# A hybrid decoder layer on one core: the linear attention's q and k turned by VectorE blocks and transfers in place of TensorE, with decay products and copies given to GpSimd

## The chip, the core and the metric

The kernel runs on one core of a Trainium2 chip. The metric is device time in microseconds for one execution, the median of several runs. Before the change it is 305.76 us (three runs, 305.73 to 305.92). The engines are called as the profile calls them: PE is TensorE (PEld its weight loads), DVE is VectorE, ACT is ScalarE, POOL is GpSimd, SP is the SyncE that issues most transfers.

## What is computed

One layer of a decoder with 256 tokens and a width of 1024, all in float32. A single input projection of the normed x gives softmax-attention q, k, v (8 heads of 64), linear-attention q, k, v (4 heads, key width 64, value width 128), an output gate r and a rank-16 gate. Both attentions feed one output projection; then comes a gated feed-forward part with a causal convolution of 3 taps, and a last norm. What matters here is the gated linear attention, chunk by chunk of 64 tokens:

```python
def gla_attention(q, k, v, log_a):
    ...
    qc = to_chunks(q * (dk ** -0.5))
    kc, vc = to_chunks(k), to_chunks(v)
    G = jnp.cumsum(to_chunks(log_a), axis=3)
    ...
        diff = G_[:, :, :, None, :] - G_[:, :, None, :, :]
        decay = jnp.exp(jnp.where(causal[None, None, :, :, None], diff, -jnp.inf))
        A = jnp.einsum('bhtd,bhsd,bhtsd->bhts', q_, k_, decay)
        o = (jnp.einsum('bhts,bhsv->bhtv', A, v_)
             + jnp.einsum('bhtd,bhdv->bhtv', q_ * jnp.exp(G_), state))
```

The result o is normed per head (so a common factor on it matters only through a small epsilon), multiplied by a gain and by silu(r).

## The kernel before

**Weights.** Every weight matrix comes in pieces ("slots") of up to 128 x 2048 by SP (L92) into a ring of four raw buffers. Each slot is split into a high part by ACT (split_hi, L99) and a low part by DVE (split_lo, L102), and each product is made of three matmuls (mm3, L115 to L118: high x high, high x low, low x high). When the last low part of a slot is written, split_lo issues the next load on SP (load_next), so loads stand in SP's queue in the order in which low parts are finished.

**Order.** PE, ACT and DVE run in the order in which the program lists their instructions; the order on SP and POOL is left to the scheduler. The input projection is a list of 48 steps of about 1.4 us on PE (for the last 24, six matmuls of 512 columns each): steps 0 to 11 the linear attention's q, k and gate ("G", slots 0, 3, 4, 5) and the first pieces of softmax q and k; 12 to 17 softmax q (slots 6, 7); 18 to 23 softmax k (slots 8, 9); 24 to 31 v (slots 10, 11); 32 to 39 the linear v (slots 12, 13); 40 to 47 r (slots 14, 15); 48 to 63 are the output projection (slots 16 to 19). Everything else hangs on the plan, a table written by hand (L631 to L653): at step q, or at its half (q + 0.5), the functions of that row are emitted, so their PE instructions stand at that place in PE's queue and their ACT and DVE instructions behind those of earlier rows. The feed-forward part behind it (22 blocks of weights) is bound by PE in the same way.

**Linear attention.** At step 12 the rows of G, with tokens on partitions, are scaled by the norm and copied to gqk (g_evac, L274): columns 0 to 255 are q, 272 to 527 k. g_lr_split (L287, L288) and g_wgs_lo (L282) prepare the gate's operands. At 14.5 g_transpose transposes q and k with eight PE instructions of 128 x 128 (L302), so that the channels lie on partitions, and ACT copies them to gqT, with the factor 1/8, and gkT (L303), and k once more to gk1 (L305). g_diag (L309, L311, L314) multiplies q and k, makes id64 and sums the products of each head on DVE; g_diag2 (L320) makes from them the diagonal of the attention matrix ATd on ACT. g_gate_mm (L325), g_gate and g_decay (L341) make the decay of each token, dec[0]. Then the triangle of a chunk is filled by levels: for b = 1, 2, 4 up to 32 lvl_u multiplies q (L355, L356, L362) and k (L363) in place by the decays of half a block, and L364 makes the decays of the next level by products of neighbours. lvl_c (L399) makes a level's products on PE and lvl_d_ (L410) copies them with a mask to ATd. Levels 0 and 1 are multiplied together at step 29; so that later levels may overwrite q and k, their operands are kept aside: q1 and gk1 for level 0, and for level 1 copies by ACT (lvl_keep, L382, L383).

**Softmax attention around it.** rope_a copies the swapped halves of q and k (ACT, L512, to the tile qs) and rope_b rotates them (DVE, L519 to L521). m_scores (L535), m_max (L557), m_exp (L564), m_div (L570 to L572) and m_pt (PE transposes of the probabilities, L581) follow for pairs of heads from step 29 on. masks (L541 to L545) loads and copies the causal mask.

**The form that the change reuses.** In the feed-forward part the kernel already turns a tile by 32 x 32 blocks on DVE (blocks, L913) and then moves whole blocks between partitions by transfers of SP (to_rows, L920), 16 of 32 partitions by 16 runs of 128 bytes.

Of the kernel before, what the change touches and what calls it, by code (L numbers as in the profile page):

```python
# [9 lines left out]
F32 = mybir.dt.float32  # L10
# [24 lines left out]
def trunk_kernel(ctx: ExitStack, tc: tile.TileContext, xT_d, wG_d, w5_d, wo_d, up_d, dn_d,  # L35
# [174 lines left out]
    gqT = at.tile([128, 2, S], F32, name="gqT")  # L210
    gkT = at.tile([128, 2, S], F32, name="gkT")
# [18 lines left out]
    gr = at.tile([128, 2, 512], F32, name="gr")  # L230
# [65 lines left out]
    def g_transpose(which):  # L296
        p = att()
        o, dst, sc = ((0, gqT, DK ** -0.5), (272, gkT, 1.0))[which]
        for pr in range(2):
            for tt in range(2):  # L300
                c = pr * S + tt * 128
                T.transpose(p[:, c:c + 128], gqk[:, tt, o + pr * 128:o + (pr + 1) * 128], ident)  # L302
        A.activation(dst.rearrange("p a t -> p (a t)"), p, AF.Copy, scale=sc)  # L303
        if which:
            A.activation(gk1.rearrange("p a t -> p (a t)"), p, AF.Copy)  # L305

    def g_diag():
        dgp = at.tile([128, 2, 256], F32, name="e", bufs=2)
        V.scalar_tensor_tensor(dgp, gqk[:, :, 0:256], DK ** -0.5, gqk[:, :, 272:528],  # L309
                               op0=ALU.mult, op1=ALU.mult)  # L310
        V.tensor_add(id64, ident[:, 0:64], ident[:, 64:128])  # L311
        dg = at.tile([128, 2, 2, 2], F32, name="dg")
        for tt in range(2):
            V.tensor_reduce(dg[:, :, tt, :], dgp[:, tt].rearrange("p (a h d) -> p a h d", a=2, h=2),  # L314
                            axis=mybir.AxisListType.X, op=ALU.add)
        st["dg"] = dg.rearrange("p a b c -> p (a b c)")
# [22 lines left out]
    def g_decay():  # L339
        V.tensor_sub(st["mn"], st["mn"], st["ln"])  # L340
        A.activation(dec[0], st["mn"], AF.Exp, scale=1.0 / TAU)  # L341

# [9 lines left out]
    def lvl_u(l):  # L352
        b = LEVELS[l]
        if l == 0:
            V.tensor_mul(q1, two(gqf, 1)[:, :, 1, 0], two(dec[0], 1)[:, :, 1, 0])  # L355
# [6 lines left out]
        V.tensor_mul(two(gqf, c)[:, :, 1], q, dc[:, :, 0].to_broadcast([128, n, c]))  # L362
# [812 lines left out]
```

## Time and profile before

| | |
|---|---|
| median of 3 runs | 305.76 us |
| the profiled execution | 306.11 us |
| its span, first to last instruction | 304.1 us |
| granted TensorE clock | 1.000 |
| POOL busy, instructions | 4.8 us, x21 |
| moved by SP's queue | 55.86 MB, 53.1% of 16 engines |

The profile is of one execution. A row of the timeline gives the start and the duration in us, engine, line, operation, tiles and shape, how many were merged, and in brackets the idle time in front and what ended it. A row of a line gives minimum, median and maximum in ns. The chain that ended last is followed back from the last instruction.

### The profile page before, as it was taken

How to read it: one execution, taken by the hardware profiler on the slowest of the kernel's cores; microseconds unless marked ns; L12 is line 12 of the kernel's file. 1: busy time of each engine (PE TensorE's matmuls, PEld its weight loads, DVE VectorE, ACT ScalarE, POOL GpSimd, SP SyncE). 2: the span in 40 equal slices, each digit the busy share in tenths (PEclk: the TensorE clock that was granted, in tenths of full speed). 3: DMA queues.
4: the chain of work that ended last, by engine and by line, in shares of the span. 5: the costliest groups of instructions: out<-in, count | busy, mean ns of one | idle time of the engine just before them, and what ended most of it. 6: DMA issues, size and time to landing. Idle time of an engine off the chain costs nothing.

```text
span 304.1 us, 6224 instructions
## 1 busy us (share of the span) xinstructions
PE 297.7 (98%) x2470; PEld 282.2 (93%) x2470; DVE 248.2 (82%) x464; ACT 207.0 (68%) x384; POOL 4.8 (2%) x21
## 2 busy tenths in 40 slices
PE   8999999999999999999999999999999999999992
PEld 8999988777889999999999999999999999999992
DVE  3788998999387699799999998887888788876653
ACT  3988999898998487657667775555556665534362
POOL 2020000000000000000000000000000000000000
PEclk9999999999999999999999999999999999999999
DMA  6998845274553542991567666448788622220003
GB/s 163 391 332 307 297 165 198 91 261 141 176 182 134 204 168 65 426 370 32 210 245 256 254 235 236 170 156 224 211 194 234 267 71 69 71 69 2 0 0 139
DMA packets 20892, 56.38 MB, mean 185 GB/s; under 512 B 9840, under 2 KB 11648, under 8 KB 16640
## 3 DMA queue, kind: packets, MB, share of 16 engines
q1 hardware_dynamic: 20720, 55.86, 53.1%
q8 instruction: 19, 0.31, 0.4%
q10 hardware_dynamic: 144, 0.13, 0.1%
q14 instruction: 9, 0.07, 0.1%
HBM read 53.89 MB, written 1.05 MB: 181 GB/s over the span
## 4 chain that ended last, share of the span: by engine, by line
PE 98%; ACT 0%; issue 0%; DVE 0%; ACTq 0%
PE att L116 14%; PE att L117 14%; PE att L118 14%; PE acc L116 14%; PE acc L118 14%; PE acc L117 14%; PE att L746 4%; PE acc L727 1%; PE att L77 1%; PE att L399 1%; PE att L535 1%; PE att L581 1%; PE att L463 1%; PE att L601 1%; PE acc L735 1%; PE att L302 0%
## 5 line engine op out<-in xcount | busy, mean ns | idle before, releaser
L99 ACT ACTIVATE hi<-raw 128x1024 fp32r<-128x1024 f32 (+4 forms) x87 | 79.9, 941 | 38.4 <-PE att L117 31.9
L102 DVE TENSOR_TENSOR lo<-raw,hi 128x1024 fp32r<-128x1024 f32 (+4 forms) x89 | 93.6, 1065 | 14.0 <-ACT hi L99 14.0
L116 PE MATMUL att<-hh,hi 128*128 128x256 f32 x352 | 98.4, 279 | 0.0
L117 PE MATMUL att<-hl,hi 128*128 128x256 f32 x352 | 98.3, 279 | 0.0
L118 PE MATMUL att<-hh,lo 128*128 128x256 f32 x352 | 98.2, 279 | 0.0
L116 PEld LDWEIGHTS att<-hh,hi 128*128 128x128 f32 x352 | 66.2, 188 | 0.0
L117 PEld LDWEIGHTS att<-hl,hi 128*128 128x128 f32 x352 | 66.2, 188 | 0.0
L118 PEld LDWEIGHTS att<-hh,lo 128*128 128x128 f32 x352 | 66.2, 188 | 0.0
L873 DVE SCALAR_TENSOR_TENSOR c<-us,par,c 128x256 f32<-128x256 f32 x88 | 40.7, 482 | 4.1 <-ACT c L865 2.5
L865 ACT ACTIVATE c<-us,par 128x256 f32<-128x256 f32 x44 | 24.0, 591 | 23.7 <-DVE us L855 18.4
L118 PE MATMUL acc<-dhi,gl 128*128 128x512 f32 (+1 forms) x88 | 32.1, 365 | 0.0
L117 PE MATMUL acc<-dlo,gh 128*128 128x512 f32 (+1 forms) x88 | 32.1, 365 | 0.0
L116 PE MATMUL acc<-dhi,gh 128*128 128x512 f32 (+1 forms) x88 | 31.9, 363 | 0.0
L815 DVE TENSOR_TENSOR dlo<-draw,dhi 128x1024 fp32r<-128x1024 f32 x22 | 26.6, 1218 | 0.0
L855 DVE TENSOR_TENSOR us<-att,rb 128x512 f32<-128x512 f32 x20 | 13.8, 688 | 11.5 <-PE att L118 11.5
L810 ACT ACTIVATE dhi<-draw 128x1024 fp32r<-128x1024 f32 x22 | 23.0, 1046 | 0.0
L116 PE MATMUL acc<-hi,ah 128*128 128x512 f32 x48 | 19.5, 406 | 0.0
L118 PE MATMUL acc<-hi,al 128*128 128x512 f32 x48 | 19.0, 396 | 0.0
L117 PE MATMUL acc<-lo,ah 128*128 128x512 f32 x48 | 19.0, 396 | 0.0
L117 PEld LDWEIGHTS acc<-dlo,gh 128*128 128x128 f32 x88 | 16.5, 188 | 2.0
L116 PEld LDWEIGHTS acc<-dhi,gh 128*128 128x128 f32 x88 | 16.5, 188 | 1.9
L118 PEld LDWEIGHTS acc<-dhi,gl 128*128 128x128 f32 x88 | 16.5, 188 | 1.9
(222 smaller groups left out, 511.0 us busy)
## 6 DMA issues: line engine op xcount, KB each, us to landing
raw<-in_up SPq DMA_DIRECT2D x22, 1024.0 KB, 4.9
draw<-in_dn SPq DMA_DIRECT2D x22, 512.0 KB, 5.7
raw<-in_w SPq DMA_DIRECT2D x7, 1024.0 KB, 6.8
raw<-in_wo SPq DMA_DIRECT2D x4, 1024.0 KB, 4.8
raw<-in_w SPq DMA_DIRECT2D x4, 512.0 KB, 5.6
raw<-in_wG SPq DMA_DIRECT2D x3, 528.0 KB, 5.8
raw<-in_w SPq DMA_DIRECT2D x4, 256.0 KB, 5.4
xg<-hB SPq DMA_DIRECT2D x16, 64.0 KB, 6.4
```

Of the source, the lines that this page charges most:

```text
L77: T.matmul(wp[:, :w], zero, zero[:, :w], start=True, stop=True)
L99: A.activation(self.hi[:, a:b], self.raw[:, a:b], AF.Copy)
L102: V.tensor_sub(self.lo[:, a:b], self.raw[:, a:b], self.hi[:, a:b])
L116: T.matmul(out, sh, mh, start=first, stop=False, **kw)
L117: T.matmul(out, sh, ml, start=False, stop=False, **kw)
L118: T.matmul(out, sl, mh, start=False, stop=last, **kw)
L746: T.matmul(st["G"][tt][c][:, :c1 - c0], sta[:, k, tt * 128:(tt + 1) * 128], mov[:, kk, c0:c1], start=k == 0 and i == 0, stop=k == KT - 1 a ...
L810: A.activation(hi, downs[i][0], AF.Copy)
L815: V.tensor_sub(lo, d, hi)
L855: V.tensor_tensor(u[:, :, 2:], upo[i][2].rearrange("p (a t) -> p a t", a=2), rb[:, None, :].to_broadcast([128, 2, S]), op=ALU.mult)
L865: A.activation(cv[i][:, a], u[:, a, 2:], AF.Identity, bias=par[:, P_CB + m:P_CB + m + 1], scale=par[:, P_CW + 2 * 2 * NP + m:P_CW + 2 * 2 ...
L873: V.scalar_tensor_tensor(c[:, a], u[:, a, w:w + S], par[:, wc:wc + 1], c[:, a], op0=ALU.mult, op1=ALU.add)
```

## The change

- q and k are turned by two DVE block transposes into gB (g_blocks) and 16 transfers of 32 x 32 blocks into gT (g_turn), even ones on SP's queue, odd ones on POOL's. gqT and gkT are views of gT. The eight PE transposes and ACT's copies of L303 and L305 go; gk1 is copied by POOL (g_keep1).
- q isn't scaled any more; the factor 1/8 goes into the evacuation of the linear v (a DVE instruction makes the scaled norm factors), as the diagonal's products, too, lose it.
- The decay products of all levels move from DVE (L364, L371) to POOL, right behind dec[0]; the kept copies of level 1 (lvl_keep) move from ACT to POOL; the diagonal's multiplication and id64 move from DVE to POOL, and its sums (g_diag1) stay on DVE but move from step 14.5 to 24.
- gB and gr share a buffer (tag "gr").
- The plan is rearranged: g_wgs_lo goes behind slot 7's last low part, the gate from 15.5 to 16, level 0 behind slot 9's last low part, k's half of level 1 to step 20, the loads of lvl and masks from 12.5 to 19, slot 11's second high part to step 24.

```diff
+    def g_blocks():
+        for w, o in enumerate((0, 272)):
+            V.transpose(gB[:, w].rearrange("p r a f -> p a r f"),
+                        gqk[:, :, o:o + 256].rearrange("p a (r f) -> p a r f", r=2))
+
+    def g_turn():
+        src = gB.rearrange("p w r a f -> p (w r a) f")
+        dst = gT.rearrange("p w r (a t) -> p (w r a) t", a=2)
+        for n in range(16):
+            b, c = divmod(n, 4)
+            (nc.gpsimd if n % 2 else DMA).dma_start(dst[32 * b:32 * b + 32, :, 32 * c:32 * c + 32], src[32 * c:32 * c + 32, :, 32 * b:32 * b + 32])
+
+    def g_keep1():
+        nc.gpsimd.tensor_copy(gk1.rearrange("p a t -> p (a t)"), gkf)
...
-        V.scalar_tensor_tensor(dgp, gqk[:, :, 0:256], DK ** -0.5, gqk[:, :, 272:528],
-                               op0=ALU.mult, op1=ALU.mult)
-        V.tensor_add(id64, ident[:, 0:64], ident[:, 64:128])
+        nc.gpsimd.tensor_mul(dgp, gqk[:, :, 0:256], gqk[:, :, 272:528])
+        nc.gpsimd.tensor_add(id64, ident[:, 0:64], ident[:, 64:128])
...
     def g_decay():
         V.tensor_sub(st["mn"], st["mn"], st["ln"])
         A.activation(dec[0], st["mn"], AF.Exp, scale=1.0 / TAU)
+        for l in range(1, 7):
+            dc = two(dec[l - 1], 1)
+            nc.gpsimd.tensor_mul(dec[l], dc[:, :, 0, 0], dc[:, :, 1, 0])
...
     def lvl_keep():
         q, k = keep(1)
-        A.activation(q.rearrange("p (n b) -> p n b", b=2), two(gqf, 2)[:, :, 1], AF.Copy)
-        A.activation(k, gkf, AF.Copy)
+        nc.gpsimd.tensor_copy(q.rearrange("p (n b) -> p n b", b=2), two(gqf, 2)[:, :, 1])
+        nc.gpsimd.tensor_copy(k, gkf)
...
     def gv_evac(tt):
-        A.activation(gv[:, tt], st["gv"][tt], AF.Copy, scale=rstd(tt))
+        if tt == 0:
+            V.tensor_scalar(rsx[:, 2:4], rsx[:, 0:2], DK ** -0.5, None, op0=ALU.mult)
+        A.activation(gv[:, tt], st["gv"][tt], AF.Copy, scale=rsx[:, 2 + tt:3 + tt])
...
-            (12, lambda: do((xnorm, lambda: slots[7].split_lo(0, 512)), (lambda: slots[7].split_lo(512, 1024),), (g_evac, 0), (g_lr_split,), (g_evac, 1), (g_wgs_lo,), (hi, 7, 1), (lo, 7, 1))),
-            (12.5, lambda: do((DMA.dma_start, lvl, lvl_d), (masks,))),
+            (12, lambda: do((xnorm, lambda: slots[7].split_lo(0, 512)), (lambda: slots[7].split_lo(512, 1024),), (g_evac, 0), (g_lr_split,), (g_evac, 1), (g_blocks,), (g_turn,), (hi, 7, 1), (lo, 7, 1), (g_wgs_lo,))),
             (13.5, lambda: do((hi, 8, 0))),
-            (14.5, lambda: do((g_transpose_lr,), (g_transpose, 0), (g_transpose, 1), (xrow,), (lo, 8, 0), (g_diag,))),
-            (15.5, lambda: do((g_gate_mm,), (g_gate,), (hi, 9, 0), (g_decay,), (lo, 9, 0), (hi, 9, 1))),
-            (16.5, lambda: do((lvl_u, 0), (lo, 9, 1), (lvl_u, 1))),
-            (18, lambda: do((rope_a, 0, 0), (rope_b, 0, 0), (hi, 10, 0), (lo, 10, 0), (rope_a, 0, 1), (rope_b, 0, 1), (hi, 10, 1), (lo, 10, 1))),
-            (20, lambda: do((hi, 11, 0), (lo, 11, 0), (hi, 11, 1), (lvl_keep,), (DMA.dma_start, glag, gla_g_d))),
-            (24, lambda: do((lvl_u, 2), (rope_a, 1, 0), (rope_b, 1, 0), (lo, 11, 1), (rope_a, 1, 1), (rope_b, 1, 1), (hi, 12, 0), (lo, 12, 0), (g_diag2, 0), (g_diag2, 4))),
+            (14.5, lambda: do((g_transpose_lr,), (xrow,), (lo, 8, 0))),
+            (16, lambda: do((g_gate_mm,), (g_gate,), (hi, 9, 0), (g_decay,), (lo, 9, 0), (hi, 9, 1), (g_keep1,), (g_diag,))),
+            (18, lambda: do((lo, 9, 1), (lvl_u, 0), (lvl_u, 1, (0,)), (rope_a, 0, 0), (rope_b, 0, 0), (hi, 10, 0), (lo, 10, 0), (rope_a, 0, 1), (rope_b, 0, 1), (hi, 10, 1), (lo, 10, 1))),
+            (19, lambda: do((DMA.dma_start, lvl, lvl_d), (masks,), (DMA.dma_start, glag, gla_g_d))),
+            (20, lambda: do((hi, 11, 0), (lvl_u, 1, (1,)), (lvl_keep,), (lo, 11, 0))),
+            (24, lambda: do((lvl_u, 2), (rope_a, 1, 0), (rope_b, 1, 0), (hi, 11, 1), (lo, 11, 1), (rope_a, 1, 1), (rope_b, 1, 1), (hi, 12, 0), (lo, 12, 0), (g_diag1,), (g_diag2, 0), (g_diag2, 4))),
```

In lvl_u the new argument parts picks q's multiplication (0), k's (1) or both.

More of the change, by code (lines that the diff above doesn't have):

```diff
@@ L209, in trunk_kernel @@
     gqk = at.tile([128, 2, NG], F32, name="gqk")
-    gqT = at.tile([128, 2, S], F32, name="gqT")
-    gkT = at.tile([128, 2, S], F32, name="gkT")
+    gT = at.tile([128, 2, 2, S], F32, name="gT")
+    gqT, gkT = gT[:, 0], gT[:, 1]
+    gB = at.tile([128, 2, 2, 2, 128], F32, name="gB", tag="gr")
     gk1 = at.tile([128, 2, S], F32, name="gk1")
@@ L229, in trunk_kernel @@
     gv = at.tile([128, 2, 512], F32, name="gv")
-    gr = at.tile([128, 2, 512], F32, name="gr")
     glag = at.tile([128, 512], F32, name="glag")
@@ L294, in g_transpose_lr, with g_diag1 @@
         A.activation(lrT, p[:, :S], AF.Copy)
[L296 to L305, printed above, removed]
+    def g_blocks():
[10 more added lines that the diff above has]
+        nc.gpsimd.tensor_copy(gk1.rearrange("p a t -> p (a t)"), gkf)
     def g_diag():
         dgp = at.tile([128, 2, 256], F32, name="e", bufs=2)
-        V.scalar_tensor_tensor(dgp, gqk[:, :, 0:256], DK ** -0.5, gqk[:, :, 272:528],
-                               op0=ALU.mult, op1=ALU.mult)
-        V.tensor_add(id64, ident[:, 0:64], ident[:, 64:128])
+        nc.gpsimd.tensor_mul(dgp, gqk[:, :, 0:256], gqk[:, :, 272:528])
+        nc.gpsimd.tensor_add(id64, ident[:, 0:64], ident[:, 64:128])
+        st["dgp"] = dgp
+    def g_diag1():
+        dgp = st["dgp"]
         dg = at.tile([128, 2, 2, 2], F32, name="dg")
@@ L350, in two, with lvl_u @@
         return x.rearrange("p (n two b) -> p n two b", two=2, b=b)
-    def lvl_u(l):
+    def lvl_u(l, parts=(0, 1)):
         b = LEVELS[l]
@@ L361, in lvl_u @@
         q = q1.rearrange("p (n c) -> p n c", c=1) if l == 1 else two(gqf, c)[:, :, 1]
-        V.tensor_mul(two(gqf, c)[:, :, 1], q, dc[:, :, 0].to_broadcast([128, n, c]))
-        V.tensor_mul(two(gkf, c)[:, :, 0], two(gkf, c)[:, :, 0], dc[:, :, 1].to_broadcast([128, n, c]))
-        V.tensor_mul(dec[l], dc[:, :, 0, 0], dc[:, :, 1, 0])
+        if 0 in parts:
+            V.tensor_mul(two(gqf, c)[:, :, 1], q, dc[:, :, 0].to_broadcast([128, n, c]))
+        if 1 in parts:
+            V.tensor_mul(two(gkf, c)[:, :, 0], two(gkf, c)[:, :, 0], dc[:, :, 1].to_broadcast([128, n, c]))
     def lvl_u64():
@@ L370, in lvl_u64 @@
         V.tensor_mul(two(gkf, c)[:, :, 0], two(gkf, c)[:, :, 0], dc[:, :, 1].to_broadcast([128, 8, c]))
-        V.tensor_mul(dec[6], dc[:, :, 0, 0], dc[:, :, 1, 0])
         d6 = dec[6].rearrange("p (a b c) -> p a b c", a=2, b=2)
@@ L490, in g_gated @@
         y = st["y", tt]
-        V.tensor_mul(y, y, gr[:, tt])
+        V.tensor_mul(y, y, st["gr"][:, tt])
     def g_out():
```

4 lines of the change are left out of this document (3 added, 1 removed).

## The prediction

> **What bounds the kernel now.** I read the page first, then the chain of waits in order of time, then who waited for whom on TensorE, then the timeline of each engine from 20 to 62 us, where the change acts.
>
> ```profile
> span 304.1 us, 6224 instructions
> PE 297.7 (98%) x2470; PEld 282.2 (93%) x2470; DVE 248.2 (82%) x464; ACT 207.0 (68%) x384; POOL 4.8 (2%) x21
> PE 98%; ACT 0%; issue 0%; DVE 0%; ACTq 0%
> PE att L77 <- PEq L1164: 0.8, 1, 0.8
> ```
>
> The third line is the chain that ended last: it is TensorE (PE) almost alone. The fourth is the only wait that the profile has for matmuls on PE, at the launch. So PE runs without a hole from the first matmul to the end. Time can be gained only by taking instructions from PE, and any hole put into PE is lost for good, because nothing behind it has slack to give back. I therefore keep one number through the working: s, by how much PE is later than before (negative: earlier). The s that PE has when the attention part is over is the change of the total.
>
> **What leaves PE.** Before, q and k of the linear attention are transposed by eight PE instructions (L302). They stand between two others:
>
> ```profile
> 26.99 1.06 PE L302 MATMUL att<-ident,gqk 128*128 128x128 f32 x8
> 27.89 0.38 PE L265 MATMUL att<-ident,rsx 128*128 128x128 f32 x2
> 29.51 0.40 PE L325 MATMUL att<-lrT,wgs 128*128 128x256 f32 x2
> 29.75 0.28 PE L116 MATMUL acc<-ah,hi 128*128 128x256 f32 x1
> 29.87 0.28 PE L117 MATMUL acc<-al,hi 128*128 128x256 f32 x1
> ```
>
> From 26.99 to 27.89 is 0.90 us: s can become -0.90 and no better. That alone is 0.29% of the time. Everything else in the change can only hide or cost.
>
> **What VectorE gets in exchange, and the first wait.** The blocks are turned by two VectorE (DVE) instructions, each of the form that the kernel already has at L913:
>
> ```profile
> 25.95 0.23 DVE L288 TENSOR_TENSOR lrs<-gqk,lrs 128x64 fp32r<-128x64 f32 x1
> 26.21 0.85 DVE L282 TENSOR_TENSOR wgs<-wgu,wgs 16x256 fp32r<-16x256 f32 x2
> 27.34 1.23 DVE L102 TENSOR_TENSOR lo<-raw,hi 128x1024 fp32r<-128x1024 f32 x1 [0.28 <-ACT hi L99]
> L913 DVE STREAM_TRANSPOSE hB<-xg x4: 703/704/707, 175.3 to 199.1; 128x512 f32<-128x512 f32 x4
> ```
>
> They start where L282 stood, at 26.2, and end at 26.2 + 2 x 0.70 = 27.6. The low part of slot 7 follows (1.2, to 28.75), and only then, because the change moves it to the end of the list, L282 (0.85, to 29.6). L282 writes the wgs that the gate's matmul L325 reads. That matmul moves from half step 15.5 to step 16, six matmuls of 0.117 later (the last two rows are 0.12 apart), so with 0.90 less in front PE would reach it at 29.51 + 0.70 - 0.90 = 29.31. It waits 0.25 for wgs: s = -0.65. The cover that L282 had before (PE was 2.4 us behind it) is gone.
>
> **The 16 transfers.** Each moves 32 partitions by 8 runs of 128 bytes, half of what one transfer of L920 moves in such runs. Eight are issued by the SP queue, eight by GpSimd (POOL).
>
> ```profile
> L920 SPq DMA_DIRECT2D xg<-hB x16: 597/720/847, 202.2 to 229.2; - x16
> DMA to landing us min/median/max: 5.7/6.4/7.3
> out_y<-yy SPq DMA_DIRECT2D x3, 128.0 KB, 1.9
> 15.57 13.35 SPq L92 DMA_DIRECT2D raw<-in_w  x6
> 28.97 2.51 SPq L627 DMA_DIRECT2D lvl<-in_lvl  x1
> raw<-in_w SPq DMA_DIRECT2D x7, 1024.0 KB, 6.8
> ```
>
> SP: 8 x 0.72 from 27.6, the last issued at 32.6. Landing lies between 1.9 (nothing in front) and 6.4 (L920, which is issued right behind two loads of weights). Here no load is issued right in front: the next one of SP's, the last of the six in L92's row, stands behind them. So I take 2.5, near the low end: all of SP's half is there at 35.1. POOL: the trace has no transfer issued by GpSimd. Its price lies between 0.6 (L920's shortest) and the 2.5 of L627; I take L920's 0.72, the same kind of runs, which again gives 35.1. The ends give 27.6 + 7 x 0.6 + 1.9 = 33.7 and 27.6 + 7 x 2.5 + 6.4 = 51.5.
>
> The Trainium skill, "DMA: Bandwidth & Descriptors", Specifications, puts a GpSimd-issued DMA's first byte at about 1 us and a SyncE-issued one's at about 0.6. If each issue took that 1 us, an estimate, the last of q and k would land at 37.1, and the sum below would be +0.6 in place of -0.1; no row here shows a GpSimd issue.
>
> Raw loads: the one for slot 11, issued at about 28.6 before, now stands behind eight issues (to 33.4) and lands at 40.2 by the 6.8 of its kind; ScalarE (ACT) reads it at about 41.5. Nothing on the path, but a cover of 6 us shrinks to 1. The transfers of lvl, causal and glag, with GpSimd's two copies for the masks, move to step 19: SP's 2.5 for lvl no longer stands in front of slot 12's load, and their first reader is the softmax behind 53, so they cost nothing.
>
> **When DVE needs q and k.** The first reader, level 0 of the decay (L355, L356), moves behind the low part of slot 9, second half. From there to the rotation of the second q half DVE has this to do:
>
> ```profile
> 34.38 0.42 DVE L355 TENSOR_TENSOR q<-gqT,dec 128x256 f32<-128x256 f32 x1
> 37.40 0.69 DVE L519 TENSOR_TENSOR mqT<-acc,cos 128x512 f32<-128x512 f32 x1
> 39.34 1.22 DVE L102 TENSOR_TENSOR lo<-raw,hi 128x1024 fp32r<-128x1024 f32 x1
> 40.91 0.69 DVE L519 TENSOR_TENSOR mqT<-acc,cos 128x512 f32<-128x512 f32 x1 [0.36 <-ACT qs L512]
> 33.36 0.64 ACT L341 ACTIVATE dec<-d 128x512 f32<-128x512 f32 x1 [0.38 <-DVE d L340]
> ```
>
> At 40.91 DVE waits for ACT, not for its own work. ACT is early by about 0.37 now, since DVE's diagonal work (a multiplication, id64, the two sums of L314) no longer stands in front of the gate and ACT's wait of 0.38 at L341 goes; ACT's three copies of q and k (L303, L305) go too but only turn into waiting for the gate's matmul. So the second q half can be rotated from 40.55. Backwards: 0.68 for level 0, 0.38 for q of level 1, 1.94 for the first rotation, 1.13 for a low part, 4.1 together: q and k may land up to 36.4 at no cost. DVE itself gets to level 0 at about 35.5 (34.38 before, and one low part of 1.13 now in front), so 35.1 costs nothing and there is 0.9 to spare. Later than 36.4 pushes all that follows on DVE (rotations, low parts, level 2), one for one.
>
> **GpSimd's products and copies.**
>
> ```profile
> 0.92 0.52 POOL L223 MEMSET ATf<- 64x512 f32 x1
> 1.49 0.31 POOL L224 MEMSET wgs<- 128x256 f32 x1
> 19.17 1.64 POOL L690 CAST identr<-ident 128x128 fp32r<-128x128 f32 x1 [16.15 <-DMA ident<-in_ident]
> 36.10 0.65 POOL L545 COPY causal<-causal 64x64 f32<-64x64 f32 x2 [15.29 <-DMA causal<-in_causal]
> ```
>
> The memsets give 0.85 ns an element, the copies 0.32 for 64 elements, so 0.25 + 0.85 ns an element is my estimate; by the cast it would be 12.8 ns. Six products, the kept k and the diagonal are about 3.5 us, due only by 43.9, 7 us after they can start. On the path is lvl_keep, 768 elements, 1.1 us (9.8 by the cast): it can start after k of level 1 at 44.0, lies under the low part of slot 11 (1.13), and level 2 on DVE waits for it. I charge 0.2. What ACT and DVE lose here (1.0 us of copies at L382/L383, 1.1 of products) hides nothing that was late.
>
> **What is late next.** The two sums L314 now stand on DVE at the end of the list of step 24, behind the low part of slot 12, and ACT's eight products into ATd (L320) wait for them. Behind these on ACT's queue stand the high part of slot 12, the softmax exponentials and the divisions.
>
> ```profile
> 42.84 2.35 DVE L102 TENSOR_TENSOR lo<-raw,hi 128x1024 fp32r<-128x1024 f32 x2
> 52.15 1.22 DVE L102 TENSOR_TENSOR lo<-raw,hi 128x1024 fp32r<-128x1024 f32 x1
> 31.02 0.73 DVE L314 TENSOR_REDUCE dg<-e 128x4 f32<-128x256 f32 x2
> 50.52 2.01 ACT L320 ACTIVATE ATd<-id,dg 128x64 f32<-128x64 f32 x8
> 52.44 1.04 ACT L99 ACTIVATE hi<-raw 128x1024 fp32r<-128x1024 f32 x1
> 53.61 0.40 ACT L564 ACTIVATE pe<-pe,mx 128x128 f32<-128x128 f32 x1
> 55.29 0.19 ACT L564 ACTIVATION_READ_ACCUMULATOR pe<-pe,mx 128x1 f32 x1
> 56.54 0.87 ACT L571 ACTIVATE pe<-pe,mx 128x128 f32<-128x128 f32 x2 [1.06 <-DVE mx L570]
> 58.51 0.59 PE L581 MATMUL att<-ident,pe 64*128 64x64 f32 x12
> 60.06 0.40 PE L117 MATMUL acc<-lo,ah 128*128 128x512 f32 x1
> ```
>
> DVE from 40.55: three rotations 3 x 1.94, four low parts 4 x 1.13, k of level 1 0.38, the wait 0.2, level 2 0.67, the sums 0.73: 12.3 us, so they end at R = 52.9. Before, L320 ran from 50.52, under DVE's work; now ACT stands idle from about 49 to R. Then L320 1.92, the high part 1.04, four exponentials with their sums 1.87 (first and last row), the first division 0.45: the first probabilities are ready at R + 5.3 = 58.2 and the second at R + 5.75. PE's L581 takes them at 58.51 + s and 58.77 + s, so s is at least -0.3 and -0.1. DVE's low part of slot 12, second half, comes behind the second division, at R + 7.1 = 60.0, and PE's first use was 60.06: -0.1 again. Sum: s = -0.90 + 0.25 + 0.55 = -0.1. Behind this I find no step with less slack. The scaling of q moved into gv costs one tiny DVE instruction under gv's evacuation.
>
> The profiled execution took 306.11 us for its span of 304.1; its result would be 306.0. It stands 0.35 above the median of 305.76, so of the median 305.65 is left.
>
> **The rivals.** (1) The whole gain but the first wait: R is at or below 52.3, because ACT's rotations or DVE's drains come out shorter than row by row; then -0.65, 305.1. For it: PE never waits before, and every duration is an upper one where instructions overlap. Against it: L581 had 1.1 us of slack and the reordering takes more than 2. (2) Slower: GpSimd's issue. From 0.9 us an issue on, q and k land after 36.4, DVE stands at level 0 with two low parts and two rotations behind it, and R moves with it: 1.2 us an issue is 38.5, s = +2.0, 307.75; 1.0 is +0.6. For it: L627's 2.5 on SP. Against it: L920. (3) Slower by contention on the shared work of DVE and GpSimd: if each reading GpSimd instruction holds DVE for its length, the 3.5 us of products fall on DVE between 37 and 44 and s reaches +2 to +3, about 308. The rows of L690 and L545 speak to it: the cast took 1.64 for 128 elements under busy DVE, and DVE's instruction beside L545 took this:
>
> ```profile
> 36.19 0.46 DVE L362 TENSOR_TENSOR gqT<-q,dec 128x256 f32<-128x256 f32 x1
> 45.11 0.42 DVE L362 TENSOR_TENSOR gqT<-gqT,dec 128x256 f32<-128x256 f32 x1
> ```
>
> GpSimd waits, then, and DVE loses 0.04. The Trainium skill, "SBUF — State Buffer", Who interferes with whom, says that a DVE instruction with two SBUF inputs and a GpSimd instruction that reads SBUF exclude each other for the whole instruction, whoever starts first winning; the two rows agree for GpSimd's side and show nothing for DVE's.
>
> **How the numbers follow.** A measurement here can tell about 0.2% (0.6 us) from no change. The forecast (s between -0.6 and +0.6): 0.40. Rival 1: 0.25, the only faster one. Rival 2: 0.25. Rival 3, with GpSimd copies much slower than estimated: 0.10. So faster 0.25, same 0.40, slower 0.35. The range goes from 305.0 (rival 1) to 308.2 (GpSimd's issue at 1.25 us); about 0.07 is left out below and 0.12 above. The forecast's own range is 305.1 to 306.4.
>
> **What would show it.** Right: L302 gone; a PE wait of 0.2 to 0.3 at L325 on DVE's wgs; level 0 on DVE at about 35.5 with no wait for a DMA; ACT idle some 4 us before L320, ended by DVE's dg; a PE wait at L581 or on the low part of slot 12 near 58 to 60. Wrong: level 0 waiting for a DMA beyond 36.4 (rival 2), long DVE low parts between 37 and 45 (rival 3), or no wait at L581 and R below 52.3 (rival 1).

## The result and the profile after

The changed kernel takes 308.39 us (median of 6 runs, 307.83 to 308.76), the kernel before on the same chip 305.93 (6 runs, 305.73 to 306.17). The ratio is 1.008, 95% interval 1.0067 to 1.0093: slower by 2.5 us, where the forecast was no change, and 0.2 above the range. The profiled execution took 308.55 for a span of 306.4.

First the page: its span and busy times, the shares of the chain that ended last, and, from the waits of PE, whom its matmuls waited for (us in total, times, longest).

```profile
span 306.4 us, 6260 instructions
PE 298.9 (98%) x2462; PEld 282.2 (92%) x2462; DVE 250.4 (82%) x459; ACT 204.6 (67%) x379; POOL 17.6 (6%) x40
PE 87%; DVE 6%; ACT 2%; DMA 2%; issue 1%; SPq 1%; ACTq 0%; DVEq 0%
```

```profile
PE acc L117 <- DVE lo L102: 0.6, 1, 0.6
PE att L595 <- DVE ATd L420: 0.2, 1, 0.2
```

PE was 98% of the chain before and is 87% now: DVE, ACT and DMA have a share. PE did give up its eight transposes (x2470 to x2462) and still lost 2.2 us. These two rows name only 0.8 of it, so I followed PE's shift itself: the start of the same matmul of L116 to L118, counted from the first, in this kernel minus that in the kernel before, less the same difference at the first one (23.27 us before; it differs between executions by up to 0.8, by when the first loads land). Negative is earlier. The columns are times in the kernel before; the experiments are told below.

| shift of PE, us, at | 28.0 | 30.5 | 44.9 | 50.8 | 59.0 | 65.1 | 130 |
|---|---|---|---|---|---|---|---|
| changed kernel | -0.89 | -0.55 | +0.53 | +1.19 | +1.48 | +1.84 | +2.08 |
| e1, GpSimd only writes | -0.89 | -0.56 | -0.55 | +0.11 | +0.11 | +0.11 | +0.36 |
| e2, turn undone | -0.01 | 0.00 | 0.00 | 0.00 | +0.69 | +1.05 | +1.30 |
| e3, sums early | -0.89 | -0.49 | +0.60 | +1.27 | +1.26 | +1.27 | +1.52 |
| e4, landing tile | -0.89 | -0.56 | +0.53 | +0.52 | +0.51 | +0.60 | +0.84 |
| e5, gate early | -0.89 | -0.86 | +0.22 | +0.22 | +0.22 | +0.30 | +0.55 |
| e6, own engines | -0.89 | -0.88 | -0.88 | -0.86 | -0.15 | +0.31 | +0.31 |
| e12, kept k late | -0.80 | -0.80 | -0.73 | -0.74 | -0.54 | -0.53 | -0.53 |

So the changed kernel gains 0.89 by the transposes, loses 0.34 at the gate, 1.08 at slot 10, 0.66 at level 2 of the decay, 0.29 and 0.36 at the first two transposes of probabilities, and 0.24 in small steps up to 130 us. Five places; the prediction had priced the first loss, and the one at the probabilities through the late sums.

A run's time is its span and a rest outside it, which the runs of one kernel mostly share within 0.1 us (e5 from 2.0 to 2.5) and the kernels don't. By the medians it is 2.0 us in the kernel before, 2.1 in the changed one and in e3, 2.4 in e4, 2.2 in e5 and 1.8 in e1, e2, e6 to e10 and e12. What sets it wasn't looked into; where it bears on a comparison below, the spans are given too.

**The transfers did what was forecast.** Rows of a line: minimum, median, maximum in ns, first and last start; below them the landing of GpSimd's.

```profile
L306 SPq DMA_DIRECT2D gT<-gB x8: 592/616/1312, 27.5 to 33.0; - x8
L306 POOL DMA_DIRECT2D gT<-gB x8: 582/583/761, 27.8 to 32.0; - x8
```

```profile
gT<-gB POOLq DMA_DIRECT2D x8, 32.0 KB, 2.5
L365 DVEq EVENT_SEMAPHORE  x8: 21/50/50, 35.6 to 36.2; - x8
```

An issue by GpSimd takes 0.58 and lands after 2.5; the last of the 16, SP's at 33.0, has landed by 35.6 (forecast 35.1). The rival of a slow issue falls. Level 0 starts at 36.33, where 35.5 was forecast: DVE's low parts in front of it end at 36.02, and DVE's queue then still executes instructions that only wait for the transfers' semaphores, eight from 35.6 to 36.2 (the last row). That is inside the 36.4 up to which the prediction called a delay free. The Trainium skill, "DMA: Bandwidth & Descriptors", Specifications, puts a GpSimd-issued transfer's first byte at about 1 us; as the price of an issue, which is how the prediction weighed it, the trace shows 0.58 instead.

**DVE is held while GpSimd reads.** The timeline of DVE and of GpSimd, start and duration first:

```profile
33.24 1.23 DVE L102 TENSOR_TENSOR lo<-raw,hi 128x1024 fp32r<-128x1024 f32 x1 [0.19 <-ACT hi L99]
34.71 1.31 DVE L102 TENSOR_TENSOR lo<-raw,hi 128x1024 fp32r<-128x1024 f32 x1 [0.24 <-ACT hi L99]
36.33 1.12 DVE L365 TENSOR_TENSOR q<-gT,dec 128x256 f32<-128x256 f32 x1 [0.31 <-issue]
37.38 0.62 DVE L366 TENSOR_TENSOR gT<-gT,dec 128x256 f32<-128x256 f32 x1
38.35 0.68 DVE L533 TENSOR_TENSOR mqT<-acc,cos 128x512 f32<-128x512 f32 x1
39.69 1.05 DVE L535 TENSOR_TENSOR mqT<-mqT,qs 128x512 f32<-128x512 f32 x1
40.66 1.44 DVE L102 TENSOR_TENSOR lo<-raw,hi 128x1024 fp32r<-128x1024 f32 x1
42.02 0.68 DVE L533 TENSOR_TENSOR mqT<-acc,cos 128x512 f32<-128x512 f32 x1
43.33 0.69 DVE L535 TENSOR_TENSOR mqT<-mqT,qs 128x512 f32<-128x512 f32 x1
45.41 1.22 DVE L102 TENSOR_TENSOR lo<-raw,hi 128x1024 fp32r<-128x1024 f32 x1
46.55 0.83 DVE L373 TENSOR_TENSOR gT<-gT,dec 128x256 f32<-128x256 f32 x1
53.76 0.74 DVE L321 TENSOR_REDUCE dg<-e 128x4 f32<-128x256 f32 x2
54.41 0.28 DVE L571 CUSTOM_DVE_ANT_0 pe<-att,causal 128x128 f32<-128x128 f32 x1
```

```profile
33.81 1.12 POOL L351 TENSOR_TENSOR dec<-dec 128x256 f32<-128x256 f32 x1 [1.20 <-ACT dec L348]
34.90 2.27 POOL L313 TENSOR_TENSOR e<-gqk 128x512 f32<-128x512 f32 x1
37.13 1.98 POOL L351 TENSOR_TENSOR dec<-dec 128x128 f32<-128x128 f32 x5
39.58 0.61 POOL L309 COPY gk<-gT 128x512 f32<-128x512 f32 x1 [0.47 <-DMA raw<-in_w]
40.13 0.88 POOL L392 COPY s<-gT 128x256 f32<-128x256 f32 x1
45.56 1.54 POOL L393 COPY dec<-gT 128x512 f32<-128x512 f32 x1 [4.55 <-DVE gT L375]
```

Read the two side by side. Level 0 (L365, L366) took 0.42 each before and takes 1.12 and 0.62 beside GpSimd's L313 and L351; the rotation's addition (L535) 1.05 beside the copy L309, and 0.69 in the next rotation, at 43.33; the low part 1.44 in place of 1.22 beside L392; level 2's q 0.83 in place of 0.42 beside L393. L533, one of whose inputs comes from PSUM (acc), keeps 0.68 beside the end of L351. The low part at 33.24 began before GpSimd's L351 and keeps 1.23; there GpSimd seems to be held, with 1.12 for 256 elements, where L313's 512 need 1.15 from the end of DVE's low part (36.02) to their own end (37.17); no row has these products beside an idle DVE. At 45.56 GpSimd was held: DVE's low part had begun at 45.41 and keeps 1.22, and the copy takes 1.54. This is what the Trainium skill, "SBUF — State Buffer", Who interferes with whom, states: a DVE instruction with two inputs in SBUF and a GpSimd instruction that reads SBUF shut each other out for the whole instruction, and the first to start wins. The trace agrees, for both sides now: +0.70, +0.20, +0.36, +0.22 and +0.41 on DVE. Not all of it fits: the low part at 34.71 began 0.19 before L313 and still takes 1.31 for 1.22.

At 42.02 DVE starts the second q rotation, forecast at 40.55: 1.47 late, as much as the first four of these losses (1.48). From there to the end of the sums at 54.41, where the next row starts, DVE needs 12.4 for a forecast 12.3.

**Who pays.** PE at slot 10's low part and at level 2, and ACT in front of the diagonal:

```profile
41.88 0.40 PE L117 MATMUL acc<-lo,ah 128*128 128x512 f32 x1
49.69 0.65 PE L399 MATMUL att<-gqT,gkT 64*64 64x32 f32 x32
50.16 0.75 PE L535 MATMUL att<-mkT,mqT 64*64 64x256 f32 x16
```

These three are PE's rows of the kernel before; in the changed kernel:

```profile
42.15 0.50 PE L117 MATMUL acc<-lo,ah 128*128 128x512 f32 x1 [0.55 <-DVE lo L102]
50.33 1.25 PE L409 MATMUL att<-gT 64*64 64x32 f32 x31
51.39 0.41 PE L549 MATMUL att<-mkT,mqT 64*64 64x256 f32 x3
59.93 0.76 PE L595 MATMUL att<-ident,pe 64*128 64x64 f32 x12
```

```profile
54.27 2.03 ACT L327 ACTIVATE ATd<-id,dg 128x64 f32<-128x64 f32 x8 [4.62 <-DVE dg L321]
```

```profile
L409 PEldq EVENT_SEMAPHORE  x8: 51/51/51, 50.1 to 50.9; - x8
```

The last row is one that nobody had priced: between 50.1 and 50.9 the queue of PE's weight loads executes eight instructions that only wait for semaphores, 51 ns each and about 0.12 from one to the next, though all that they wait for landed by 35.6. Before, the next matmuls (L535) started 0.47 after level 2's first (49.69 to 50.16); now it is 1.06 (50.33 to 51.39).

### The profile page after: what moved, and what is told of

It reads as the page before. It is cut to its first block, busy times and chain, and to the rows that moved or that the text cites. A ratio compares the mean times of both kernels' runs of the same rounds, so it can differ in the third digit from the quotient of the medians.

```text
span 306.4 us, 6260 instructions
## 1 busy us (share of the span) xinstructions
PE 298.9 (98%) x2462; PEld 282.2 (92%) x2462; DVE 250.4 (82%) x459; ACT 204.6 (67%) x379; POOL 17.6 (6%) x40
## 3 DMA queue, kind: packets, MB, share of 16 engines
q1 hardware_dynamic: 22896, 56.12, 52.9%
HBM read 53.89 MB, written 1.05 MB: 179 GB/s over the span
## 4 chain that ended last, share of the span: by engine, by line
PE 87%; DVE 6%; ACT 2%; DMA 2%; issue 1%; SPq 1%; ACTq 0%; DVEq 0%
PE att L116 14%; PE att L118 14%; PE att L117 14%; PE acc L116 12%; PE acc L117 12%; PE acc L118 12%; PE att L759 3%; DVE lo L102 3%; DMA raw<-in_w 2%; PE acc L740 1%; ACT ATd L327 1%; PE att L477 1%; PE att L615 1%; DVE qs L534 1%; ACT pe L578 1%
## 5 line engine op out<-in xcount | busy, mean ns | idle before, releaser
L116 PE MATMUL att<-hh,hi 128*128 128x256 f32 x352 | 98.4, 280 | 0.0
L117 PE MATMUL att<-hl,hi 128*128 128x256 f32 x352 | 98.3, 279 | 0.0
L118 PE MATMUL att<-hh,lo 128*128 128x256 f32 x352 | 98.2, 279 | 0.0
L117 PEld LDWEIGHTS att<-hl,hi 128*128 128x128 f32 x352 | 66.2, 188 | 0.0
L116 PEld LDWEIGHTS att<-hh,hi 128*128 128x128 f32 x352 | 66.2, 188 | 0.0
L118 PEld LDWEIGHTS att<-hh,lo 128*128 128x128 f32 x352 | 66.2, 188 | 0.0
L117 PE MATMUL acc<-dlo,gh 128*128 128x512 f32 (+1 forms) x88 | 32.2, 365 | 0.0
L118 PE MATMUL acc<-dhi,gl 128*128 128x512 f32 (+1 forms) x88 | 32.2, 365 | 0.0
L116 PE MATMUL acc<-dhi,gh 128*128 128x512 f32 (+1 forms) x88 | 32.0, 363 | 0.0
L117 PE MATMUL acc<-lo,ah 128*128 128x512 f32 x48 | 19.1, 399 | 0.6 <-DVE lo L102 0.6
L116 PE MATMUL acc<-hi,ah 128*128 128x512 f32 x48 | 19.6, 408 | 0.0
L118 PE MATMUL acc<-hi,al 128*128 128x512 f32 x48 | 19.0, 396 | 0.0
L117 PEld LDWEIGHTS acc<-dlo,gh 128*128 128x128 f32 x88 | 16.5, 188 | 2.0
L116 PEld LDWEIGHTS acc<-dhi,gh 128*128 128x128 f32 x88 | 16.5, 188 | 1.9
L118 PEld LDWEIGHTS acc<-dhi,gl 128*128 128x128 f32 x88 | 16.5, 188 | 1.9
```

The lines of the kernel that those rows point to most:

```text
L116: T.matmul(out, sh, mh, start=first, stop=False, **kw)
L117: T.matmul(out, sh, ml, start=False, stop=False, **kw)
L118: T.matmul(out, sl, mh, start=False, stop=last, **kw)
```

## The experiments

Two theories stood at the start. A: GpSimd's reads hold DVE, and what comes late by that (slot 10, the sums) reaches PE. B: the turn itself is late, by its transfers and their semaphores. The diffs are against the changed kernel unless another is named.

**e1: GpSimd only writes.**

```diff
-            nc.gpsimd.tensor_mul(dec[l], dc[:, :, 0, 0], dc[:, :, 1, 0])
+            nc.gpsimd.memset(dec[l], 0.5)
...
-        nc.gpsimd.tensor_mul(dgp, gqk[:, :, 0:256], gqk[:, :, 272:528])
+        nc.gpsimd.memset(dgp, 0.5)
```

and so for id64 and the three copies.

> The changed kernel, but GpSimd's instructions that read (the six decay products, the diagonal product, the identity's halves, the kept copies of q and k) are replaced by memsets of the same tiles: the decays past level 0, the diagonal and the kept copies are left out of the computation. Theory A (GpSimd's reads hold DVE): the DVE rows between 36 and 47 fall back to what they took before (level 0 from 1.12 and 0.62 to 0.42, L535 from 1.05 to 0.69, L102 from 1.44 to 1.22), the sums L321 end at about 52.9 in place of 54.4, and TensorE ends 1.6 to 2.2 us earlier than in the changed kernel: 306.2 to 306.8. Theory B (q and k come late by the transfers and their semaphores): the rows stay as long, the sums end near 54.4, 308.4 stays within 0.3.

Measured: 306.33 (305.95 to 307.19, 11 runs), ratio 1.0011 (1.0001 to 1.0021), 2.06 below the changed kernel (1.8 by the spans, 304.5 for 306.3). DVE of this kernel:

```profile
36.41 0.42 DVE L364 TENSOR_TENSOR q<-gT,dec 128x256 f32<-128x256 f32 x1 [0.62 <-issue]
43.90 1.22 DVE L102 TENSOR_TENSOR lo<-raw,hi 128x1024 fp32r<-128x1024 f32 x1
51.83 0.73 DVE L321 TENSOR_REDUCE dg<-e 128x4 f32<-128x256 f32 x2
```

```profile
44.10 0.53 POOL L392 MEMSET dec<- 128x512 f32 x1 [11.19 <-DVE gT L374]
```

Every DVE row is back at its old length, the low part at 43.90 too, with GpSimd's memset in the middle of it: writing alone holds nobody. The sums end at 52.48, 0.4 earlier than forecast, and PE's shift stays at -0.55 through slot 10. A holds; but the 0.66 at level 2 is still there, so part of the loss is of another kind. Level 0 starts no earlier than in the changed kernel, behind the same eight semaphore instructions and 0.62 of idle time, and nothing comes late by it.

**e2: the turn undone.**

```diff
+                T.transpose(p[:, c:c + 128], gqk[:, tt, o + pr * 128:o + (pr + 1) * 128], ident)
+        A.activation(gT[:, which].rearrange("p a t -> p (a t)"), p, AF.Copy)
...
-(g_blocks,), (g_turn,), 
```

> The changed kernel with the turn undone: q and k go through eight TensorE transposes and two ACT evacuations again, no block transposes and no transfers; GpSimd keeps all its new work and the order is the changed one. Theory A: the same DVE rows are stretched, the sums end at 54.0 to 54.4, and TensorE is 1.3 to 1.6 us later than before although it gave nothing up: 307.2 to 307.5. Theory B: without the transfers nothing is late: 305.9 to 306.3.

Measured: 307.44 (307.14 to 309.08, 6 runs), ratio 1.0056 (1.0039 to 1.0074). GpSimd's work alone, without the turn, costs 1.4 us.

```profile
36.31 0.62 DVE L361 TENSOR_TENSOR q<-gT,dec 128x256 f32<-128x256 f32 x1
45.59 0.83 DVE L369 TENSOR_TENSOR gT<-gT,dec 128x256 f32<-128x256 f32 x1
52.80 0.74 DVE L317 TENSOR_REDUCE dg<-e 128x4 f32<-128x256 f32 x2
```

```profile
58.97 0.48 PE L591 MATMUL att<-ident,pe 64*128 64x64 f32 x3 [0.46 <-DVE ATd L416]
```

Level 0 (0.62) and level 2 (0.83 for 0.42) are stretched again, the sums end at 53.45, where DVE's next row starts (forecast 54.0 to 54.4), and PE waits at the probabilities. Slot 10 is in time: PE comes there 0.55 later than in the changed kernel, and DVE's low part 1.0 earlier (39.67 for 40.66). B falls as the main cause.

**e3: the sums early.**

```diff
-(lvl_u, 2), (rope_a, 1, 0),
+(lvl_u, 2), (g_diag1,), (rope_a, 1, 0),
...
-(hi, 12, 0), (lo, 12, 0), (g_diag1,), (g_diag2, 0), (g_diag2, 4)
+(hi, 12, 0), (g_diag2, 0), (g_diag2, 4), (lo, 12, 0)
```

> The changed kernel with one move: DVE's two sums L321 stand right behind level 2 instead of at the end of their list, and ACT's eight products L327 stand between the two high parts of slot 12. Theory A with the recorded step (the products wait for the late sums, and TensorE for them): ACT's wait of 4.6 us at L327 goes, L595 no longer waits, TensorE keeps the shift of +1.3 that it had at the end of the level-2 products: 307.6 to 307.8, 0.6 to 0.8 below the changed kernel. Rival: the rotations and low parts behind the sums are what decides, the sums in front of them cost as much: 308.4 within 0.2.

Measured: 307.64 (307.46 to 307.77, 5 runs), ratio 1.0049 (1.0037 to 1.0061), 0.75 below the changed kernel. ACT's products run behind the high part with no wait:

```profile
49.55 2.00 ACT L327 ACTIVATE ATd<-id,dg 128x64 f32<-128x64 f32 x8
```

and PE's shift does not move from +1.27 between 50.8 and 65. So the step of the late sums was right in kind: the late sums cost the 0.29 and 0.36 at the probabilities, and no more, since PE was late already.

**e4: a landing tile**, on top of e3. The transfers write a tile of their own, g0 (in the buffer that the rotated k takes later); DVE's levels 0 and 1 and one ACT copy of the odd k bring q and k into gT, so that PE no longer reads anything that a transfer wrote.

```diff
-        dst = gT.rearrange("p w r (a t) -> p (w r a) t", a=2)
+        dst = g0.rearrange("p w r (a t) -> p (w r a) t", a=2)
...
+    def k_odd():
+        A.activation(two(gkf, 1)[:, :, 1, 0], two(gk0, 1)[:, :, 1, 0], AF.Copy)
```

> As the kernel with the early sums, and the 16 transfers land in a tile of their own; level 0 and level 1 on DVE write q and the even k from it into the working tile, and one ACT copy of 256 columns brings the odd k. So TensorE's level products depend on DVE and ACT and no longer on 16 transfers. If TensorE's eight additional semaphore instructions at L409 cost what they seem to (the 16 matmuls of level 2 take 1.06 us in place of 0.47): 0.5 to 0.6 below the kernel with the early sums, 307.0 to 307.2. If these waits lie beside other work of TensorE's: the same as that kernel within 0.2.

Measured: 307.33 (307.21 to 307.99, 5 runs), ratio 1.0044 (1.0032 to 1.0056). It is 0.3 below e3 by the medians, less than the 0.5 to 0.6 forecast, but 0.6 by the medians of the spans (305.5 and 304.9); what lies outside the span took 0.4 more. PE's rows:

```profile
50.28 0.65 PE L413 MATMUL att<-gT 64*64 64x32 f32 x32
50.75 0.75 PE L555 MATMUL att<-mkT,mqT 64*64 64x256 f32 x16
```

Level 2 takes 0.47 again, the eight semaphore instructions at 50 are gone, and PE's shift falls from +1.27 to +0.52. The semaphores of 16 transfers cost PE 0.66 to 0.75 in one place.

DVE's row of level 0 settles what the semaphores in front of it cost:

```profile
35.90 1.51 DVE L366 TENSOR_TENSOR q<-g,dec 128x256 f32<-128x256 f32 x1
```

Here it starts 0.43 earlier than in the changed kernel and ends at 37.41, where it ended at 37.45 there. Its end follows GpSimd's product of the diagonal, which ends at 37.13 here and at 37.17 there, and not its own start. So DVE's idle 0.31 at 36.0 cost nothing in the changed kernel.

**e5: the gate's low half early**, on top of e4.

```diff
-(hi, 7, 1), (lo, 7, 1), (g_wgs_lo,)
+(hi, 7, 1), (lo, 7, 1)
...
-(g_wgs_hi,), (hi, 7, 0)
+(g_wgs_hi,), (hi, 7, 0), (g_wgs_lo,)
```

> As the kernel with the landing tile, and DVE's two instructions for the low half of the gate's weights (L282) stand in the list of step 4 again, where DVE is idle before 23.4, so that TensorE's gate matmul finds them ready. Recorded step: that wait costs TensorE 0.25 to 0.33. Theory A: the wait goes, TensorE is 0.3 earlier up to 41 us, and then waits 0.3 longer for the low part of slot 10, because DVE's stretched rows set that: 307.0 to 307.4, no change from the landing tile's 307.33, unless DVE itself comes earlier by its 0.85. Rival: the terms add up, 0.3 below it.

Measured: 306.94 (306.81 to 307.51, 5 runs), ratio 1.0037 (1.0024 to 1.005), 0.39 below e4, though the two intervals overlap and the medians of the spans differ by 0.1 only. PE's shift is plainer: the wait at the gate is gone (-0.86 at 30.5), and the 0.3 lasts to the end, since DVE, too, comes to its low parts earlier by the moved instructions. The rival was right, the terms add.

**e6: own engines**, on top of e5. GpSimd keeps its eight issues; the diagonal, its sums and the decay products go to DVE (sums behind slot 9's last low part, where DVE waited for the transfers), the kept copies to ACT.

```diff
-        nc.gpsimd.tensor_mul(dgp, gqk[:, :, 0:256], gqk[:, :, 272:528])
+        V.tensor_mul(dgp, gqk[:, :, 0:256], gqk[:, :, 272:528])
...
-        nc.gpsimd.tensor_copy(k, gkf)
+        A.activation(k, gkf, AF.Copy)
```

> Block transposes, transfers, landing tile and early gate weights kept; everything that GpSimd was given goes back: the diagonal product, the identity's halves and the sums on DVE (in its holes before the transfers land), the decay products on DVE with their levels, the kept copies on ACT. GpSimd only issues its eight transfers. Theory A: no DVE row is stretched, no wait of TensorE is left between 24 and 67, and the 0.9 of the eight transposes stays: 305.0 to 305.6, that is 0.4 to 1.0 below the kernel before. Rival: DVE and ACT are too full for the work that they get back, L595 or the low part of slot 12 waits, 306 or more.

Measured: 306.28 (305.89 to 307.32, 12 runs), ratio 1.0017 (1.0009 to 1.0026). The time is the rival's. PE keeps the whole gain, -0.86, up to 50.8, as theory A had it, and gives it back at 56.8 and 64.7, in front of these two lines.

```profile
PE att L412 <- DVE dec L374: 0.4, 1, 0.4
PE att L600 <- DVE ATd L423: 0.3, 1, 0.3
```

```profile
44.00 0.63 ACT L396 ACTIVATE dec<-gT 128x512 f32<-128x512 f32 x1 [0.75 <-DVE dec L374]
44.66 2.40 ACT L529 ACTIVATE qs<-acc 32x512 f32<-32x512 f32 x4
```

```profile
47.09 0.69 DVE L538 TENSOR_TENSOR mkT<-acc,cos 128x512 f32<-128x512 f32 x1 [1.17 <-ACT qs L529]
```

ACT's copies of the odd k and of gk1 (before, one copy at 29.3, in front of the gate) can only start behind the transfers and stand among the rotations now; the kept k then waits 0.75 for DVE's level 1, and DVE 1.17 for ACT's third rotation. DVE waited there in the kernel before, too:

```profile
47.15 0.69 DVE L519 TENSOR_TENSOR mkT<-acc,cos 128x512 f32<-128x512 f32 x1 [1.09 <-ACT qs L512]
```

So ACT and DVE are as late as they were there, and PE, which is 0.9 earlier, runs into them.

**e7: the copies on DVE**, on top of e6: `V.tensor_copy` in place of `A.activation` for gk1 and the odd k.

> As the kernel with GpSimd's work given back, with the kept copy of k and the odd k copied by DVE instead of ACT, which thereby no longer waits for 16 transfers. If ACT (2.4 us of rotation copies four times, then the diagonal blocks) sets the softmax's start, this is up to 0.5 below that kernel; if DVE does, up to 0.5 above; if neither, the same within 0.2.

Measured: 306.96 (306.67 to 307.18, 5 runs), ratio 1.0033 (1.0022 to 1.0045): worse than e6 by 0.7, where at most 0.5 was forecast. ACT then waits 2.1 us for DVE before the kept k, and PE 0.4 at L554 for the rotated k. Which of the two engines has the copies matters less than who waits for whom.

**e8: level 1 early**, on top of e6, k of level 1 and the first decay product right behind q of level 1.

```diff
-(lvl_u, 0), (lvl_u, 1, (0,)), (rope_a, 0, 0)
+(lvl_u, 0), (lvl_u, 1), (rope_a, 0, 0)
```

> As the kernel with GpSimd's work given back to DVE and ACT, with k of level 1 and the first decay product on DVE right behind q of level 1 (as in the kernel before) instead of behind the low part of slot 10. There ACT stood idle 0.75 us in front of the kept k, and everything on ACT and DVE up to the softmax was that much later. If that chain (rotations on ACT, then on DVE, the low part, the maxima) sets the wait of L600 that cost TensorE 0.7 at 58 us: the wait shrinks to about 0, and 305.4 to 305.9. Rival: the wait is set by ACT's kept copies themselves, no change from 306.28.

**e9: the softmax's order**, on top of e8.

```diff
-(hi, 12, 1), (lvl_first,),
+(lvl_first,),
...
-(m_exp, 1), (lvl_d_, 0), (lvl_d_, 1), (lvl_u, 3), (m_div, 0), (m_div, 1), (lvl_d_, 2), (lo, 12, 1)
+(m_exp, 1), (hi, 12, 1), (lvl_d_, 0), (lvl_d_, 1), (m_div, 0), (m_div, 1), (lvl_d_, 2), (lvl_u, 3), (lo, 12, 1)
...
-(lo, 13, 1), (lvl_d_, 3)
+(lvl_d_, 3), (lo, 13, 1)
```

> As the kernel with level 1 early, and four items of the softmax's lists change places: ACT's high part of slot 12, second half, behind the first exponentials, DVE's first divisions and the mask copy of level 2 ahead of level 3's products, and the mask copy of level 3 ahead of the low part of slot 13. The bank that TensorE's transposes of the probabilities write is free only when these mask copies have read it. If the two waits at L600 (0.7 at 58, 0.5 at 64) are set by them: TensorE keeps nearly the whole 0.9 of the transposes, 305.0 to 305.4, below the kernel before. Rival: the waits come from elsewhere, the same as the kernel with level 1 early.

Measured: e8 306.65 (306.08 to 307.1, 9 runs), ratio 1.002 (1.0009 to 1.003); e9 307.16 (306.75 to 307.73, 5 runs), ratio 1.0044 (1.003 to 1.0057). Both miss. In e8 the waits at the probabilities do go, but slot 10's low part is now late (PE's shift goes from -0.82 to -0.06 there): DVE has no room in front of it. In e9 slot 10 costs 0.32, and level 3's products behind the divisions make their reader wait:

```profile
57.11 0.67 PE L412 MATMUL att<-gT 64*64 64x32 f32 x32 [0.62 <-DVE dec L374]
```

With -0.06 and +0.11 at 130 us these two should have been near 306 all the same. Their last transfers to out_y land after 3.0 us, those of e10 too, where all the other kernels have 1.9 to 2.1. What makes the last landing 1 us longer in three of the kernels wasn't found; it is why I read PE's shift, not only the time.

**e10: level 1 between**, on top of e6, and **e11**, the kernel before with the new order of the softmax alone.

```diff
-(hi, 10, 0), (lo, 10, 0), (rope_a, 0, 1)
+(hi, 10, 0), (lo, 10, 0), (lvl_u, 1, (1,)), (rope_a, 0, 1)
...
+(m_exp, 1), (hi, 12, 1), (lvl_u, 3), (lvl_d_, 0), (lvl_d_, 1), (m_div, 0), (m_div, 1), (lvl_d_, 2), (lo, 12, 1)
```

> As the kernel with GpSimd's work given back, with k of level 1 on DVE between the low part of slot 10 and the second rotation (so that neither that low part comes later, as with level 1 early, nor ACT stands idle before the kept k), the second high part of slot 12 behind the first exponentials, level 3's products ahead of the mask copies, and the mask copies of levels 2 and 3 ahead of the low parts that follow. If the three waits that were seen one by one (low part of slot 10, L600 at 58 and at 64) are all that ate the 0.9 of the transposes: TensorE passes 66 us at -0.6 to -0.9, 305.1 to 305.5, below the kernel before. Rival: the next wait takes their place, or the weight loads behind the transfers come late, 306 or more.

> The kernel before with only the softmax's order changed as in the run beside it (second high part of slot 12 behind the first exponentials, level 3's products ahead of the mask copies, these ahead of the low parts). TensorE has no wait there in the kernel before, so the order alone gives nothing: 305.9 to 306.1. If this alone gains or loses 0.3 or more, what the run beside it shows is not the turn's.

Measured: e10 306.66 (306.02 to 308.14, 12 runs), ratio 1.0023 (1.001 to 1.0036); e11 305.98 (305.5 to 306.75, 12 runs), ratio 0.9998 (0.9987 to 1.0008). e11 is as expected: the order alone gives nothing. In e10, 306 or more as its rival said, the 0.68 of DVE's two instructions appears nearly one for one as PE's loss among slot 10's first matmuls (-0.80 to -0.14), and then nothing more is lost. The low part isn't late there; DVE's second q rotation is, which frees the accumulator that PE writes next:

```profile
42.74 0.47 PE L116 MATMUL acc<-hi,ah 128*128 128x512 f32 x1 [0.35 <-DVE mqT L538]
```

**e12: the kept k late**, on top of e6 with e10's order of the softmax.

```diff
-(lvl_u, 1, (1,)), (lvl_keep,), (lo, 11, 0)
+(lvl_u, 1, (1,)), (lvl_keep, (0,)), (lo, 11, 0)
...
-(lvl_u, 2), (rope_a, 1, 0), (rope_b, 1, 0),
+(lvl_u, 2, (0,)), (rope_a, 1, 0), (rope_b, 1, 0), (lvl_keep, (1,)), (lvl_u, 2, (1,)),
```

> As the kernel with GpSimd's work given back (level 1's k behind the low part of slot 10 again), with ACT's kept k behind the third rotation's copies and k of level 2 on DVE behind that rotation, so that neither ACT (0.75 us before the kept k) nor DVE (1.17 us before the rotation) stands idle there, and with the softmax's order of the run before. Theory: TensorE keeps its 0.9 up to 51 us, as in the kernel with the work given back, and both waits at L600 are gone: 305.1 to 305.6, below the kernel before. Rival: the softmax's start is set by ACT's total work from 30 us on (four rotations, six high parts, the kept copies, the diagonal), in whatever order: 306.0 to 306.4.

Measured: 305.29 (304.58 to 306.34, 11 runs) against 305.93 (305.62 to 306.17, 15 runs), ratio 0.9978 (0.9969 to 0.9987). It beats both kernels, and the forecast of 305.1 to 305.6 holds. Of the 0.64, 0.4 are in the spans (303.5 for 303.9) and the rest outside. Its profiled execution is the slowest of its 11 runs, and its first matmul of L116 came 0.78 later than in the kernel before, as PE's first work waited for the first loads:

```profile
PE acc L747 <- ACT hi L99: 0.7, 1, 0.7
```

Counted from there, PE keeps -0.74 up to 50.8 and -0.53 to the end. So the turn by blocks and transfers gives PE its 0.8 to 0.9 us; the best arrangement found keeps 0.5 of it to the end.

## Why the prediction was wrong

- **PE bounds, and a hole in it is lost for good:** right. Each step of the table stays to the end.
- **The eight transposes, -0.90:** right, -0.89.
- **The gate's wait, +0.25:** right in kind, +0.34 measured; e5 gets it back.
- **The transfers, issue 0.72 and landing 2.5, q and k in time:** right; 0.62 and 0.58 an issue, 2.6 and 2.5 to land, and level 0 at 36.33, just inside 36.4. Rival 2 falls.
- **"GpSimd waits, then, and DVE loses 0.04": here it failed.** I took that from one row, L362 with 0.46, beside a GpSimd copy that was short (L545, 0.65 for two of 64 columns), and gave rival 3 a chance of 0.10. The change sets 8.4 us of GpSimd's reading (the six rows above) beside DVE's two-input instructions, where I had 3.5 and 1.1. DVE loses 0.70, 0.20, 0.36, 0.22 and 0.41 in the rows quoted, 1.9 together, and with that the terms "second q half at 40.55" (measured 42.02) and "R = 52.9" (measured 54.41). e1 takes the reading away: 2.06 us, 1.7 by PE's shift. e2 has the reading alone: 1.4. Rival 3 is what happened, and its sign, a long low part between 37 and 45, is there (1.44 at 40.66). That its 308 came so near is partly luck: 0.66 of the loss is semaphores, which it didn't have.
- **The late sums, s at least R - 53.0:** the late sums do reach PE, and R was wrong. With R = 54.41 the rule gives +1.41; L595 starts at 59.93 for 58.51 before, +1.42. In e2, R is 53.45 and the rule gives +0.45; L591 starts 0.46 later. That the numbers meet so closely is partly luck, as the last link is another: in e2 the profile names DVE's mask copy (ATd, L416), which stands behind the divisions, and in the changed kernel the mask copies end at 59.8 and 60.0, the second probabilities at 59.6. And e3 shows that only 0.65 is at stake, as PE had lost most of it before.
- **What I had not looked for in front of 53: slot 10's low part.** I followed DVE's lateness only to the softmax. PE's first use of that low part was at 41.88; at s = -0.55, and with this execution's first matmul 0.11 later, that is 41.44, and L117 starts at 42.15: 0.71. The next three matmuls stand 0.34, 0.36 and 0.31 apart in place of 0.23, which makes 1.03 of the 1.08. The second of these steps, up to 42.85, is DVE's lateness in another row: PE starts there 0.15 behind the end of the rotation at 42.02 (0.68 long), as in e10 0.14 behind its own, where the profile names it.
- **What no step had: semaphores on PE.** I counted the 16 transfers' issues and landings, not that every engine that reads what they wrote executes waits for them: 0.66 us on PE, as e4 shows. DVE has eight, too, in front of level 0, which cost nothing here.
- **"Lvl_keep: I charge 0.2":** 0.41 on DVE's L373, and GpSimd's copy took 1.54 in place of 1.1.

What stays open: the 0.24 that builds up evenly between 95 and 121 us in the changed kernel and in e1 to e5, and not in e6 to e12; the last landing of 3.0 us in e8 to e10; and the time outside the span, which differs between kernels by up to 0.7.

## What to carry to other kernels

Work is not moved off a busy VectorE by giving two-input or copy work to GpSimd that runs at the same time: look for VectorE rows that get longer, not for GpSimd's own time. When a transfer takes the place of an engine's instruction, count the semaphores that each reader then waits for, on the bounding engine first, and let the transfers land in a tile that only an engine with slack reads. And when an instruction leaves the bounding engine, follow each late result to its first reader on that engine, the nearest one first, at the new, earlier time.

## What the runs showed of the hardware

- A semaphore wait that was satisfied long ago still takes 51 ns in the queue of PE's weight loads, and the next starts about 0.12 us after it; eight of them among the small matmuls of level 2 cost 0.59 to 0.75 us.
- Who begins first decides who is held: GpSimd's copy of 128 x 512 took 0.61 where it began before DVE's addition (39.58 and 39.69) and 1.54 where it began behind a low part (45.56 and 45.41). A memset of that size took 0.53 and held nobody.
- A GpSimd-issued transfer of 32 KB was as quick as SP's: 0.58 and 0.62 to issue, 2.5 and 2.6 to land.
